# Out-projection of a hybrid decoder trunk: PSUM banks opened with the residual, and a sixth pair of K tiles by seven products

## Chip, cores and metric

The kernel runs on one core of a Trainium2 chip. The metric is device microseconds of one launch, the median of several runs. The engines are TensorE (PE; its weight loads PEld), VectorE (DVE), ScalarE (ACT), GpSimd (POOL), and SyncE (SP), which issues nearly all DMAs.

## What is computed

Two layers, 256 tokens, width 2048, all in float32. In each layer (the reference, cut to what matters):

```python
h  = rmsnorm(x, attn_norm_g[l])
P  = h @ w_in[l]                       # q | k | v | gate_B | gate_C | conv_in
A  = differential_attention(...)       # 8 heads, 1024 columns
Cv = gate_B * short_conv(gate_C * conv_in)         # 1024 columns
x  = x + concat([A, Cv]) @ w_out[l]    # 2048 x 2048
x  = x + relu(rmsnorm(x, mlp_norm_g[l]) @ w_up[l]) ** 2 @ w_down[l]
```

## The kernel before

Tokens make two tiles of 128 (t = 0, 1), output columns make chunks of 512. A float32 product is made of three products of rounded halves (high·high, high·low, low·high: `TERMS`). Each weight tile is therefore loaded raw by SP, rounded to a high part by ScalarE (`whi`) and subtracted to a low part by VectorE (`wlo`). Raw tiles have four buffers (`RAW`), the pairs `whi`/`wlo` three, and `Weights.take` makes tiles three jobs ahead of their use (`AHEAD`).

The out-projection has K = 2048, in 8 pairs of K tiles (i = 0 to 7; 0 to 3 are attention, 4 to 7 convolution). It is done in two halves of the output columns: `left` (chunks 0 and 1) and `right` (chunks 2 and 3). A pair of K tiles and two chunks against two token tiles is a 2x2 by 2x2 block product. It is done in one of two ways:

- *ordinary*, by `pair`: each half is an entry (chunk, i) of the order list, one weight tile of 128 x 2 x 512 and 2 K tiles x 2 token tiles x 3 terms = 12 matmuls of 512 columns; both chunks take 24;
- *by seven*, by `product`: seven products of three matmuls instead of eight, on sums and differences of the blocks. The activations' sums are made once by `sums_of` (`sv`, then high and low part, `sf` or `sg`); the weights' sums by `BySeven.jobs`: two raw tiles, `w7b` and half a `whi`/`wlo` from them directly, four differences `w7t`, of which two give `w7x` and two `w7y`. Each such tile again has a high part from ScalarE and a low part from VectorE. VectorE's operations for one seven are L916, L917, L921, L922 (`w7t`) and four low parts of L880.

The seven products collect in banks `prods[1]` to `prods[7]`; `prods[2]`, `prods[3]`, `prods[4]` and `prods[8]` are also the four places of the output (chunk, token tile) = (0,0), (1,0), (0,1), (1,1), on which the ordinary halves collect. After the last seven `results` combines the banks: ScalarE copies product 1 (L972), VectorE adds (L973 to L976). Its inner `add` (L980) adds four results to the residual `xs` later; a last step adds the four output banks to it (L1061 on the left, L1167 on the right).

The order of the work on TensorE is that of the program (a manual schedule for TensorE alone). On the left it follows the list `LEFT`: columns of the gate ("c", i), the first four products of a seven ("a", i), its last three ("b", i), and ordinary halves (chunk, i). On the right it is `RIGHT`, where ("s", i) is a whole seven. On VectorE, ScalarE and SP a scheduler sets the order; each engine then runs its queue in order. The right half is followed by the MLP, whose weights come by L1284 (`uraw`, 1 MB each from w_up) and L1302 (`draw`).

Of the kernel before, what the change touches and what calls it, by code (L numbers as in the profile page):

```python
# [9 lines left out]
F32 = mybir.dt.float32  # L10
F32R = mybir.dt.float32r
AF = mybir.ActivationFunctionType
# [3 lines left out]
P = 128  # L16
# [3 lines left out]
NT = S // P  # L20
# [8 lines left out]
CH = 512  # L29
# [28 lines left out]
TERMS = ((0, 0), (0, 1), (1, 0))  # L58
# [75 lines left out]
def trunk(ctx: ExitStack, tc: tile.TileContext, x, w_in, w_out, conv_w, q_norm_g, k_norm_g,  # L134
          lambda_q1, lambda_k1, lambda_q2, lambda_k2, subln_g, attn_norm_g, mlp_norm_g,
          w_up, w_down, rel_bias, selector, out):
    nc = tc.nc
# [696 lines left out]
    A11, A21, A12, A22, S1, S2, S3, S4 = range(8)  # L834

    class BySeven:
# [9 lines left out]
        def sums_of(self, i, a11, a21, a12, a22):  # L846

            if i < self.rooms_of:
                if i % 2 == 0 or not self.rooms:
                    room = self.pool.tile([P, 2, 2, 4, P], F32R, tag="b", name="sf")  # L850
                    self.rooms = [room[:, 0], room[:, 1]]
                hi, lo = (self.rooms[i % 2][:, part] for part in range(2))
            else:
                hi, lo = (self.tmp.tile([P, 4, P], F32R, tag="s", name="sg", bufs=2)
                          for _ in range(2))
            self.sums[i] = hi, lo
            v = wide(f"sv{i}").rearrange("p (s c) -> p s c", c=P)
            nc.vector.tensor_add(v[:, 0], a21, a22)
# [4 lines left out]
            nc.vector.tensor_sub(lo, v, hi.bitcast(F32))  # L863
# [74 lines left out]
        def product(self, n, i, a, b, start, stop):  # L938

            for m, (pa, pw) in enumerate(TERMS):  # L940
                nc.tensor.matmul(self.prods[n], self.form(i, pa, a), b[pw],  # L941
                                 start=(start and m == 0), stop=(stop and m == 2))

        def pair(self, i, chunks, starts=(), last=False):

            for n, accs in chunks:
                hi, lo = self.weights.take()
                for j in range(2):
                    k = 2 * i + j
                    a = self.cat[k // KG]  # L950
                    while not a.ready:
                        work.tick()
                    steps = [(t, pa, pw) for t in range(NT) for pa, pw in TERMS]
                    if self.weights.ramp and self.weights.used == 1 and j == 0:
                        steps = [(t, pa, pw) for pa, pw in ((0, 0), (1, 0), (0, 1))
                                 for t in range(NT)]
                    for t, pa, pw in steps:
                        nc.tensor.matmul(  # L958
                            accs[t], a.ap[:, pa, k % KG, t * P:(t + 1) * P], (hi, lo)[pw][:, j],
                            start=(j == 0 and (pa, pw) == (0, 0) and (n, t) in starts),  # L960
                            stop=(last and j == 1 and (pa, pw) == TERMS[-1]))
                    work.tick()

        def results(self, n):


            prods = self.prods
            x11, x21, x12, x22 = (xs[n + m][:, t] for m in range(2) for t in range(NT))
            room = self.tmp.tile([P, 2, CH], F32, tag="ao", name="es", bufs=1)
            e1, e2, e3 = room[:, 0], wide("e2"), room[:, 1]  # L970
            e4 = self.kpool.tile([P, CH], F32, tag="kL", name="es4")
            nc.scalar.activation(e1, prods[1], AF.Copy)  # L972
            nc.vector.tensor_add(e2, prods[6], e1)  # L973
            nc.vector.tensor_add(e4, prods[5], e2)
            nc.vector.tensor_add(x22, prods[5], x22)
            nc.vector.tensor_add(e3, prods[7], e2)  # L976

            def add():
                for x_, e in ((x11, e1), (x21, e3), (x12, e4), (x22, e3)):
                    nc.vector.tensor_add(x_, x_, e)  # L980

            return add

        def left_jobs(self, w_gate, col, w):

# [12 lines left out]
        def left(self, acts, cv):  # L998
# [21 lines left out]
            def banks():  # L1020
                for a, b in ((1, 6), (2, 3)):
                    w2 = mm.tile([P, NT, CH], F32, tag="mm2", name=f"po{l}{a}")
                    prods[a], prods[b] = w2[:, 0], w2[:, 1]
                for n in (5, 7, 4):
                    prods[n] = bank(f"po{l}{n}")

            for j, (what, i) in enumerate(LEFT):
                start, end = i == SEVEN_LEFT[0], i == SEVEN_LEFT[-1]
                rest = {w for w, _ in LEFT[j + 1:]}
                if what == "c":  # L1030
                    column(i)
                elif what == "a":
                    if start:
                        banks()
                    b11, b21, b22 = weights.take()
                    self.t1, self.t3 = weights.take()
                    self.product(1, i, A11, b11, start, end)
                    self.product(2, i, A12, b21, start, not {"a", 0} & rest)
                    self.product(3, i, S4, b22, start, not {"a", 1} & rest)
                    self.product(5, i, S1, self.t1, start, end)  # L1040
                    work.tick()
                elif what == "b":
                    t2, t4 = weights.take()
                    self.product(7, i, S3, self.t3, start, end)
                    self.product(6, i, S2, t2, start, end)
                    self.product(4, i, A22, t4, start, not {"b", 0} & rest)
                    work.tick()
                    if end:
                        add = self.results(0)
                else:  # L1050
                    opening = what == 1 and 8 not in prods
                    if opening:
                        prods[8] = ps.tile([P, CH], F32, tag="av", name=f"po{l}8", bufs=1)
                    accs = ((prods[2], prods[4]), (prods[3], prods.get(8)))
                    self.pair(i, [(what, accs[what])], [(1, 1)] if opening else (),
                              not {what, "b"} & rest)
# [88 lines left out]
        def right(self, norm):  # L1145

            weights, l = self.weights, self.l
            both = [mm.tile([P, NT, CH], F32, tag="mm2", name=f"o{l}{n}") for n in (2, 3)]
            accs = [[acc[:, t] for t in range(NT)] for acc in both]
            self.prods = prods = {2: accs[0][0], 4: accs[0][1], 3: accs[1][0]}  # L1150
            opened, add = set(), None

            for j, (what, i) in enumerate(RIGHT):
                rest = {w for w, _ in RIGHT[j + 1:]}
                if what == "s":
                    self.seven(i, i == SEVEN_RIGHT[0], i == SEVEN_RIGHT[-1], rest)
                    if i == SEVEN_RIGHT[-1]:
                        add = self.results(2)
                    continue
                first = what not in opened  # L1160
                opened.add(what)
                self.pair(i, [(what, accs[what])],
                          [(what, t) for t in range(NT)] if first else (),
                          not {"s", what} & rest)
                if not {"s", what} & rest:
                    for t in range(NT):
                        nc.vector.tensor_add(xs[2 + what][:, t], accs[what][t], xs[2 + what][:, t])  # L1167
                    if add is not None:
                        add()
                        add = None  # L1170
                    work.start(norm.chunk(2 + what, 2), 0 if what else 2)


# [579 lines left out]
```

## Time and profile before

| what | value |
|---|---|
| runs | 2112.37, 2112.66, 2113.86 us; median 2112.66 |
| span of the profiled execution | 2110.7 us |
| TensorE busy | 2105.2 us, at full granted clock throughout |
| VectorE, ScalarE, GpSimd busy | 1834.6, 1407.5, 189.4 us |
| left half from the first seven on, layer 1 | 251.8 to 336.6 us |
| right half, layer 1 | 336.6 to 375.2 us |

The profile shows one execution; its span runs from the first to the last instruction, and no other time of that execution is given. The runs' times contain what lies around the span. In rows of instructions the first number is the start and the second the duration, both in us; square brackets hold the idle time ahead of an instruction and what ended it. Rows of groups give the busy time in all, the mean in ns, and the idle time ahead.

### The profile page before, as it was taken

The page shows a single profiled execution, that of the slowest core. Times are in us where ns is not written, and L with a number is a line of the kernel's source. Part 1 is how long each engine was busy: PE and PEld are TensorE (multiplying, and loading weights), DVE is VectorE, ACT ScalarE, POOL GpSimd, SP SyncE. Part 2 cuts the span into 40 slices and gives each one's busy share as a digit, 9 for nine tenths or more (in the row PEclk, how much of TensorE's full clock was granted, in tenths as well). Part 3 has the DMA queues.
Part 4 walks back from the last instruction along what each step waited for, and adds up shares of the span by engine and source line. Part 5 has one row for each costly group of instructions (what it writes and reads, how often), then busy time and mean ns, then how long its engine had stood idle before and what let it go on. Part 6 is the DMA issues. An engine that isn't in the chain of part 4 may idle for free.

```text
span 2110.7 us, 29252 instructions
## 1 busy us (share of the span) xinstructions
PE 2105.2 (100%) x10809; PEld 1799.0 (85%) x10809; DVE 1834.6 (87%) x2525; ACT 1407.5 (67%) x1823; POOL 189.4 (9%) x226
## 2 busy tenths in 40 slices
PE   9999999999999999999999999999999999999999
PEld 7888888888888888888888888888888888888887
DVE  7888788898888888799888887988988888888998
ACT  6777566676776766666566775657676677675664
POOL 2211120000000000011101121000000000000110
PEclk9999999999999999999999999999999999999999
DMA  7655575887777777789566456668777777777993
GB/s 265 205 154 167 171 216 182 289 259 229 230 238 229 231 232 230 251 291 310 171 220 188 152 170 185 195 193 290 255 238 229 229 230 238 230 229 260 315 309 113
DMA packets 312607, 476.01 MB, mean 226 GB/s; under 512 B 12723, under 2 KB 209669, under 8 KB 312464
## 3 DMA queue, kind: packets, MB, share of 16 engines
q1 hardware_dynamic: 284752, 406.76, 60.7%
q0 software_dynamic: 27520, 67.24, 10.1%
q8 instruction: 85, 1.39, 0.3%
q14 instruction: 58, 0.48, 0.1%
q10 hardware_dynamic: 192, 0.15, 0.0%
HBM read 440.52 MB, written 33.58 MB: 225 GB/s over the span
## 4 chain that ended last, share of the span: by engine, by line
PE 98%; DMA 1%; POOL 1%; DVE 1%; issue 0%; ACT 0%; ACTq 0%; DVEq 0%
PE upc L1427 31%; PE pr L1470 14%; PE dn L1551 8%; PE gc L481 4%; PE ci L481 4%; PE gb L433 4%; PE v L456 3%; PE q L958 3%; PE o L958 3%; PE k L958 3%; PE dn L1470 3%; PE po L941 2%; PE dn L1645 2%; PE pr1r L1470 2%; PE pr0r L1470 2%; PE po L958 2%
## 5 line engine op out<-in xcount | busy, mean ns | idle before, releaser
L1427 PE MATMUL upc<-nT,uhi 128*128 128x512 f32 x1920 | 454.7, 389 | 0.0
L1427 PEld LDWEIGHTS upc<-nT,uhi 128*128 128x128 f32 x1920 | 360.2, 188 | 74.7
L1292 DVE TENSOR_TENSOR ulo<-uraw,uhi 128x1024 fp32r<-128x1024 f32 x256 | 312.3, 1222 | 109.8 <-ACT f L1459 91.5
L341 ACT ACTIVATE whi<-raw 128x1024 fp32r<-128x1024 f32 x232 | 244.7, 1058 | 180.2 <-issue 21.8
L1291 ACT ACTIVATE uhi<-uraw 128x1024 fp32r<-128x1024 f32 x256 | 270.6, 1057 | 135.7 <-PE upc L1427 115.4
L342 DVE TENSOR_TENSOR wlo<-raw,whi 128x1024 fp32r<-128x1024 f32 x232 | 284.3, 1234 | 53.1 <-ACT whi L341 46.9
L1427 PEld LDWEIGHTS upc<-nT,ulo 128*128 128x128 f32 x1920 | 246.2, 191 | 9.4
L1427 PE MATMUL upc<-nT,ulo 128*128 128x256 f32 x1920 | 249.1, 283 | 0.0
L1317 ACT ACTIVATE bh<-draw 128x1536 fp32r<-128x1536 f32 x86 | 128.3, 1492 | 103.7 <-PE pr L1470 82.1
L1318 DVE TENSOR_TENSOR bl<-draw,bh 128x1536 fp32r<-128x1536 f32 x86 | 151.3, 1759 | 11.4 <-ACT bh L1317 10.9
L1551 PE MATMUL dn<-whi,fb 128*128 128x512 f32 x480 | 152.0, 389 | 0.0
L1470 PE MATMUL pr<-bh,f 128*128 128x512 f32 x360 | 121.4, 391 | 0.0
L341 ACT ACTIVATE whi<-uraw 128x1024 fp32r<-128x1024 f32 x60 | 63.7, 1062 | 72.0 <-PE dn L1551 58.5
L1437 ACT ACTIVATE ev<-upc 128x512 f32<-128x512 f32 x120 | 72.0, 600 | 54.0 <-PE upc L1427 54.0
L1317 ACT ACTIVATE t24h<-t 128x1024 fp32r<-128x1024 f32 x86 | 91.4, 1063 | 23.7 <-PE pr L1470 15.9
L1551 PEld LDWEIGHTS dn<-whi,fb 128*128 128x128 f32 x480 | 90.1, 188 | 18.6
L1318 DVE TENSOR_TENSOR t24l<-t,t24h 128x1024 fp32r<-128x1024 f32 x86 | 104.9, 1220 | 0.2
L1330 DVE TENSOR_TENSOR t<-draw 128x1024 f32<-128x1024 f32 x86 | 105.0, 1221 | 0.1
L1318 DVE TENSOR_TENSOR t13l<-t,t13h 128x1024 fp32r<-128x1024 f32 x86 | 104.9, 1220 | 0.0
L1317 ACT ACTIVATE t13h<-t 128x1024 fp32r<-128x1024 f32 x86 | 91.5, 1063 | 8.1 <-DVE t L1330 2.9
L1470 PE MATMUL pr<-t13h,f 128*128 128x512 f32 x240 | 93.8, 391 | 0.0
L1551 PE MATMUL dn<-wlo,fb 128*128 128x512 f32 x240 | 93.4, 389 | 0.0
(528 smaller groups left out, 4383.9 us busy)
## 6 DMA issues: line engine op xcount, KB each, us to landing
uraw<-in_w_up_dram SPq DMA_DIRECT2D x128, 1024.0 KB, 6.3
raw<-in_w_in_dram SPq DMA_DIRECT2D x191, 512.0 KB, 4.2
draw<-in_w_down_dram SPq DMA_DIRECT2D x180, 512.0 KB, 5.3
raw<-in_w_out_dram SPq DMA_DIRECT2D x64, 512.0 KB, 4.5
uraw<-in_w_down_dram SPq DMA_DIRECT2D x60, 512.0 KB, 6.8
hid0p<-f POOLq DMA_DIRECT2D x17, 512.0 KB, 3.5
fb<-hid0p POOLq DMA_DIRECT2D x17, 512.0 KB, 8.0
hid1p<-f POOLq DMA_DIRECT2D x17, 512.0 KB, 3.5
```

The lines of the kernel that those rows point to most:

```text
L341: pair = (nc.scalar.activation(hi, raw, AF.Copy), nc.vector.tensor_sub(lo, raw, hi.bitcast(F32)))
L342: nc.vector.tensor_sub(lo, raw, hi.bitcast(F32)))
L481: nc.tensor.matmul(acc[:, f, 0] if part else acc[:, f], wt[:, k % 4, fs], a.ap[:, 0, k % KG] if part else a.ap[:, :, k % KG], start=(part ...
L958: nc.tensor.matmul(accs[t], a.ap[:, pa, k % KG, t * P:(t + 1) * P], (hi, lo)[pw][:, j], start=(j == 0 and (pa, pw) == (0, 0) and (n, t) in ...
L1291: pair = (nc.scalar.activation(hi, src, AF.Copy), nc.vector.tensor_sub(lo, src, hi.bitcast(F32)))
L1292: nc.vector.tensor_sub(lo, src, hi.bitcast(F32)))
L1317: keep(nc.scalar.activation(hi, src, AF.Copy))
L1318: keep(nc.vector.tensor_sub(lo, src, hi.bitcast(F32)))
L1330: keep(nc.vector.tensor_sub(t[:, 0:2], raw[:, 0::2], raw[:, 1::-1]))
L1427: nc.tensor.matmul(acc[:, 0] if part else acc, wt[part][:, k], a.ap[:, 0, k % KG] if part else a.ap[:, :, k % KG], start=(part == 0 and kh ...
L1470: nc.tensor.matmul(prods[n], f[:, pa, a], b[pw], start=(start and m == 0), stop=(stop and m == 2))
L1551: nc.tensor.matmul(prods[p], f[:, pa, 2 * k + t], b[pw][:, n], start=(p in starts and k == 0 and m == 0), stop=(stop and k == 1 and m == 2))
```

## The change

Two things are changed. First, the output banks are opened with the residual: a new `seed` has ScalarE copy `xs` into the bank, and all matmuls on it accumulate (no `start`). On the left these are the places of `prods[2]`, `prods[3]` and `prods[8]`, on the right all four. The additions of the residual in `results` go, as does its `add`; results are written to `xs` directly, and the last four additions stay. Second, pair 5 of the left half moves from two ordinary halves to a seven. The seven's last parts now stand among the ordinary halves of pairs 6 and 7. `sums_of` makes the sums of pair 5 in a room of `tmp` that the temporaries of `results` had.

```diff
 LEFT = (("c", 0), ("a", 0), ("c", 1), ("b", 0), ("c", 2), ("a", 1), ("c", 3), ("b", 1),
         ("c", 4), ("a", 2), ("c", 5), ("b", 2), ("c", 6), ("a", 3), ("c", 7), ("b", 3),
-        (0, 5), (1, 5), ("a", 4), ("b", 4), (0, 6), (1, 6), (0, 7), (1, 7))
+        (0, 6), (1, 6), ("a", 4), ("b", 4), (0, 7), ("a", 5), ("b", 5), (1, 7))
...
+            elif i % 2:
+                room = self.tmp.tile([P, 2, 4, P], F32R, tag="ao", name="so", bufs=1)
+                hi, lo = (room[:, part] for part in range(2))
             else:
...
+        def seed(self, *places):
+
+            for n, t, acc in places:
+                nc.scalar.activation(acc, xs[n][:, t], AF.Copy)
 
         def results(self, n):
...
-            room = self.tmp.tile([P, 2, CH], F32, tag="ao", name="es", bufs=1)
-            e1, e2, e3 = room[:, 0], wide("e2"), room[:, 1]
-            e4 = self.kpool.tile([P, CH], F32, tag="kL", name="es4")
-            nc.scalar.activation(e1, prods[1], AF.Copy)
-            nc.vector.tensor_add(e2, prods[6], e1)
-            nc.vector.tensor_add(e4, prods[5], e2)
-            nc.vector.tensor_add(x22, prods[5], x22)
+            e2, e3 = wide("e2"), x21 if n else wide("e3")
+            nc.scalar.activation(x11, prods[1], AF.Copy)
+            nc.vector.tensor_add(e2, prods[6], x11)
+            nc.vector.tensor_add(x12, prods[5], e2)
             nc.vector.tensor_add(e3, prods[7], e2)
-
-            def add():
-                for x_, e in ((x11, e1), (x21, e3), (x12, e4), (x22, e3)):
-                    nc.vector.tensor_add(x_, x_, e)
-
-            return add
+            nc.vector.tensor_add(x22, prods[5], e3)
+            if not n:
+                nc.vector.tensor_add(x21, x21, e3)
...
+                self.seed((0, 0, prods[2]), (1, 0, prods[3]))
...
                         prods[8] = ps.tile([P, CH], F32, tag="av", name=f"po{l}8", bufs=1)
+                        self.seed((1, 1, prods[8]))
...
                     if j == len(LEFT) - 1:
-                        add()
                         for n in range(2):
                             for t in range(NT):
                                 nc.vector.tensor_add(xs[n][:, t], accs[n][t], xs[n][:, t])
...
+            for n in range(2):
+                self.seed(*((2 + n, t, accs[n][t]) for t in range(NT)))
```

The order on the engines changes too. On VectorE, in layer 1, the end of the weights' work for the right half's first seven stood so before (`w7t` and `w7y` belong to that seven, the `wlo` of 128x1024 to ordinary halves, `nT` to the normalised input of the MLP; in the changed kernel lines behind 850 have numbers that differ by up to 4, here by 3):

```order
L921 TENSOR_TENSOR w7t<-w7t,raw 128x512
L880 TENSOR_TENSOR w7x<-w7t,w7x 128x1024
L880 TENSOR_TENSOR wlo<-raw,whi 128x512
L309 SCALAR_TENSOR_TENSOR nT_1_3582<-tpn_0_3587,gains,nT_1_3582 128x256 x2
L922 TENSOR_TENSOR w7t<-raw,w7t 128x512
L309 SCALAR_TENSOR_TENSOR nT_1_3582<-tpn_1_3610,gains,nT_1_3582 128x256 x2
L342 TENSOR_TENSOR wlo<-raw,whi 128x1024
L880 TENSOR_TENSOR w7y<-w7t,w7y 128x1024
L342 TENSOR_TENSOR wlo<-raw,whi 128x1024
```

and on the same engine at the same place it stands so now:

```order
L924 TENSOR_TENSOR w7t<-w7t,raw 128x512
L342 TENSOR_TENSOR wlo<-raw,whi 128x1024
L883 TENSOR_TENSOR w7x<-w7t,w7x 128x1024
L883 TENSOR_TENSOR wlo<-raw,whi 128x512
L309 SCALAR_TENSOR_TENSOR nT_1_3600<-tpn_0_3605,gains,nT_1_3600 128x256 x2
L925 TENSOR_TENSOR w7t<-raw,w7t 128x512
L309 SCALAR_TENSOR_TENSOR nT_1_3600<-tpn_1_3628,gains,nT_1_3600 128x256 x2
L342 TENSOR_TENSOR wlo<-raw,whi 128x1024 x2
L883 TENSOR_TENSOR w7y<-w7t,w7y 128x1024
```

The ordinary low part that stood behind `w7y`, of the half (0, 5), now stands ahead of it.

On VectorE at the end of the left half of layer 1 it stands so now around the sixth seven (`po_2771` and the like are banks, `x_84` and `x_85` the residual of the two chunks):

```order
L883 TENSOR_TENSOR w7x<-w7t,w7x 128x1024
L925 TENSOR_TENSOR w7t<-raw,w7t 128x512
L342 TENSOR_TENSOR wlo<-raw,whi 128x1024
L883 TENSOR_TENSOR w7y<-w7t,w7y 128x1024
L342 TENSOR_TENSOR wlo<-raw,whi 128x1024
L981 TENSOR_TENSOR e_3463<-po_2771,x_84 128x512
L982 TENSOR_TENSOR x_85<-po_2773,e_3463 128x512
L983 TENSOR_TENSOR e_3464<-po_2774,e_3463 128x512
```

The low part ahead of `w7y` is that of the half (0, 0) of the right. In the kernel before no seven stands there; its last left seven was followed by four ordinary halves.

On SP, from the last raw tiles of the left half of layer 1 to the MLP's first ones, it stood so before (`raw` of L383 is a tile of an ordinary half, `raw` of L895 one of a seven):

```order
L383 DMA raw<-in_w_out_dram 128x2x512 x10
L895 DMA raw<-in_w_out_dram 128x2x512 x2
L383 DMA raw<-in_w_out_dram 128x2x512 x2
L895 DMA raw<-in_w_out_dram 128x2x512 x2
L383 DMA raw<-in_w_out_dram 128x2x512 x4
L1284 DMA uraw<-in_w_up_dram 128x8x256 x5
L1302 DMA draw<-in_w_down_dram 128x1024 x6
```

and on SP it stands so now, from the two raw tiles of the sixth left seven:

```order
L898 DMA raw<-in_w_out_dram 128x2x512 x2
L383 DMA raw<-in_w_out_dram 128x2x512 x6
L1282 DMA uraw<-in_w_up_dram 128x8x256 x2
L383 DMA raw<-in_w_out_dram 128x2x512
L898 DMA raw<-in_w_out_dram 128x2x512 x2
L383 DMA raw<-in_w_out_dram 128x2x512 x2
L898 DMA raw<-in_w_out_dram 128x2x512 x2
L383 DMA raw<-in_w_out_dram 128x2x512 x4
L1282 DMA uraw<-in_w_up_dram 128x8x256 x3
```

Two of the MLP's loads moved ahead of 11 raw tiles of the right half, among them those of both its sevens.

More of the change, by code (lines that the diff above doesn't have):

```diff
@@ L941, in product @@
                 nc.tensor.matmul(self.prods[n], self.form(i, pa, a), b[pw],
-                                 start=(start and m == 0), stop=(stop and m == 2))
+                                 start=(start and m == 0), stop=(stop and m == 2),
+                                 skip_group_check=True)
         def pair(self, i, chunks, starts=(), last=False):
@@ L960, in pair @@
                             start=(j == 0 and (pa, pw) == (0, 0) and (n, t) in starts),
-                            stop=(last and j == 1 and (pa, pw) == TERMS[-1]))
+                            stop=(last and j == 1 and (pa, pw) == TERMS[-1]),
+                            skip_group_check=True)
                     work.tick()
+        def seed(self, *places):
+            for n, t, acc in places:
+                nc.scalar.activation(acc, xs[n][:, t], AF.Copy)
         def results(self, n):
@@ L1037, in left @@
                     self.product(1, i, A11, b11, start, end)
-                    self.product(2, i, A12, b21, start, not {"a", 0} & rest)
-                    self.product(3, i, S4, b22, start, not {"a", 1} & rest)
+                    self.product(2, i, A12, b21, False, not {"a", 0} & rest)
+                    self.product(3, i, S4, b22, False, not {"a", 1} & rest)
                     self.product(5, i, S1, self.t1, start, end)
@@ L1048, in left @@
                     if end:
-                        add = self.results(0)
+                        self.results(0)
                 else:
@@ L1053, in left @@
                         prods[8] = ps.tile([P, CH], F32, tag="av", name=f"po{l}8", bufs=1)
+                        self.seed((1, 1, prods[8]))
                     accs = ((prods[2], prods[4]), (prods[3], prods.get(8)))
-                    self.pair(i, [(what, accs[what])], [(1, 1)] if opening else (),
-                              not {what, "b"} & rest)
+                    self.pair(i, [(what, accs[what])], (), not {what, "b"} & rest)
                     if j == len(LEFT) - 1:
-                        add()
                         for n in range(2):
@@ L1150, in right @@
             self.prods = prods = {2: accs[0][0], 4: accs[0][1], 3: accs[1][0]}
-            opened, add = set(), None
+            for n in range(2):
+                self.seed(*((2 + n, t, accs[n][t]) for t in range(NT)))
             for j, (what, i) in enumerate(RIGHT):
@@ L1157, in right @@
                     if i == SEVEN_RIGHT[-1]:
-                        add = self.results(2)
+                        self.results(2)
                     continue
[L1160 to L1164, printed above, removed]
+                self.pair(i, [(what, accs[what])], (), not {"s", what} & rest)
                 if not {"s", what} & rest:
```

3 lines of the change are left out of this document (removed).

## The prediction

> **What bounds the kernel now.** I read the page first: its span, busy times, granted clock and chain of waits.
>
> ```profile
> span 2110.7 us, 29252 instructions
> PE 2105.2 (100%) x10809; PEld 1799.0 (85%) x10809; DVE 1834.6 (87%) x2525; ACT 1407.5 (67%) x1823; POOL 189.4 (9%) x226
> PEclk9999999999999999999999999999999999999999
> PE 98%; DMA 1%; POOL 1%; DVE 1%; issue 0%; ACT 0%; ACTq 0%; DVEq 0%
> ```
>
> TensorE is busy for the whole span at the full granted clock, and the chain that ended last is TensorE. The median of the runs, 2112.66 us, is the span plus 1.96; I take that offset as constant and add changes of the span to the median. A measurement can tell about 0.2% (4.2 us) from no change.
>
> Next, TensorE's waits over the whole program, all four that there are:
>
> ```profile
> PE warm L189 <- DVE mhalf L181: 1.1, 1, 1.1
> PE q L958 <- ACT whi L368: 0.4, 1, 0.4
> PE tpb L570 <- DMA x<-in_x_dram: 0.2, 1, 0.2
> PE k00tp L688 <- DVE ke L660: 0.2, 1, 0.2
> ```
>
> None is in the out-projection, so no wait there can be removed. Then the busy time of each engine (window, its length, then TensorE, its weight loads, VectorE, ScalarE, GpSimd) in the left half from the first seven to the end, and in the right half, for each layer:
>
> ```profile
> 251.80:336.60 84.80, 84.80 (x436) 72.53 (x435) 78.23 (x110) 50.16 (x63) 13.66 (x1) 1.00 0.63 195
> 336.60:375.20 38.60, 38.60 (x179) 31.98 (x178) 33.22 (x43) 23.87 (x35) 0.00 (x0) 1.00 0.60 187
> 1301.00:1385.70 84.70, 84.70 (x435) 72.64 (x435) 78.69 (x110) 49.58 (x62) 1.88 (x1) 1.00 0.64 196
> ```
>
> TensorE fills both. VectorE has 84.80 − 78.23 = 6.6 us to spare on the left, 5.4 on the right; ScalarE has 35. So a matmul saved is time saved, and VectorE is the engine to watch.
>
> **Fewer matmuls.** A seven is 7 products of 3 matmuls, 21; an ordinary pair is 2 chunks of 12, 24. One more pair by seven saves 3 matmuls a layer, 6 in all. Their price, and the need of the first seven on the right, are read from its rows on TensorE:
>
> ```profile
> 354.58 0.39 PE L958 MATMUL o<-whi,cat 128*128 128x512 f32 x1
> 354.81 0.84 PE L941 MATMUL po0r<-w7b,cat 128*128 128x512 f32 x3
> 356.85 1.52 PE L941 MATMUL po0r<-w7x,sf 128*128 128x512 f32 x6
> 358.21 0.84 PE L941 MATMUL po0r<-w7y,sf 128*128 128x512 f32 x3
> ```
>
> Six matmuls begin in 358.21 − 356.85 = 1.36 us, 0.227 each (the 0.39 is a duration that overlaps the next). This kernel is bound by that spacing, so the gain is 6 × 0.227 = 1.36 us. The Trainium skill, "TensorE: Matmul & The Clock Gate", section "Back-to-back issue gap", gives about 131 ns a matmul of 512 columns in a sustained stream, by which the gain would be an estimated 0.8 us; the 0.227 of this trace decides.
>
> **More work for VectorE on the left.** What a seven costs there is read from the second one on the right, whose operations follow each other:
>
> ```profile
> 358.67 0.69 DVE L916 TENSOR_TENSOR w7t<-raw 128x512 f32<-128x512 f32 x1 [1.03 <-DMA raw<-in_w_out_dram]
> 363.96 1.22 DVE L342 TENSOR_TENSOR wlo<-raw,whi 128x1024 fp32r<-128x1024 f32 x1
> 365.24 1.23 DVE L880 TENSOR_TENSOR w7y<-w7t,w7y 128x1024 fp32r<-128x1024 f32 x1
> 366.38 1.22 DVE L342 TENSOR_TENSOR wlo<-raw,whi 128x1024 fp32r<-128x1024 f32 x1
> L858 DVE TENSOR_TENSOR sv<-ay 128x128 f32<-128x128 f32 x8 | 2.3, 289 | 0.0
> L863 DVE TENSOR_TENSOR sg<-sv,sg 128x512 fp32r<-128x512 f32 x2 | 1.4, 684 | 0.0
> ```
>
> From 358.67 to 366.38 are 7.71 us, with one ordinary low part (363.96 to 365.24, 1.28) among them: 6.43 for a seven. It replaces two ordinary low parts of 1.13 (start to start, rows below): +4.17. Pair 5 now needs its sums: four of 0.29 and one of 0.68, +1.84. Three additions of 128x512 go (12 become 9), each 0.60 from start to start:
>
> ```profile
> 326.59 0.69 DVE L973 TENSOR_TENSOR e<-po,es 128x512 f32<-128x512 f32 x1
> 327.19 0.69 DVE L980 TENSOR_TENSOR x<-x,es 128x512 f32<-128x512 f32 x1
> 325.23 0.60 ACT L972 ACTIVATE es<-po 128x512 f32<-128x512 f32 x1 [0.44 <-PE po L941]
> ```
>
> That is −1.8, together +4.2 of VectorE's 6.6 − 0.7 (the left is 3 matmuls shorter): 1.7 us remain. On the right four additions go, −2.4. On average it fits, and costs nothing while its queue runs ahead of need; if that cover is gone, what misses is paid one to one.
>
> **The seeds.** ScalarE gains 7 copies of 128x512 a layer into banks, which no row here shows. The nearest is the copy out of a bank above, 0.60, so 4.2 us on an engine with 35 to spare. Bounds: nothing, or all that stands between a bank's release and its first matmul. The tight one is the right half's first bank: the sixth product ends 15 matmuls (3.40 us) before the left ends; ahead of the seeds may stand one low part (1.13), one addition (0.60) and two copies (1.2), 2.9. I take nothing, with 0.5 to spare. The other seeds have more.
>
> **The two tight places.** The order of VectorE now puts an ordinary low part ahead of the last one (w7y) of the sixth left seven and of the right's first seven. That low part waits for ScalarE's high part, which waits for TensorE to release its buffer at the start of the seven. Before, it stood behind w7y:
>
> ```profile
> 355.06 1.06 ACT L341 ACTIVATE whi<-raw 128x1024 fp32r<-128x1024 f32 x1 [0.51 <-PE o L958]
> 346.52 0.68 DVE L916 TENSOR_TENSOR w7t<-raw 128x512 f32<-128x512 f32 x1
> 354.15 1.22 DVE L342 TENSOR_TENSOR wlo<-raw,whi 128x1024 fp32r<-128x1024 f32 x1
> 355.28 1.22 DVE L880 TENSOR_TENSOR w7y<-w7t,w7y 128x1024 fp32r<-128x1024 f32 x1
> 341.29 1.23 DVE L342 TENSOR_TENSOR wlo<-raw,whi 128x1024 fp32r<-128x1024 f32 x1 [1.97 <-ACT whi L341]
> 340.21 1.04 ACT L341 ACTIVATE whi<-raw 128x1024 fp32r<-128x1024 f32 x1
> ```
>
> The release lets ScalarE start 0.25 after the seven's first matmul (355.06 against 354.81); high part 1.06; hand-over 0.04 (341.25 to 341.29); low part 1.13; w7y 1.22: 3.70 us. TensorE wants w7y's low part with the second matmul on it, the 17th, after 16 × 0.227 = 3.63. What a hand-over to TensorE costs shows at the left's last seven, where VectorE is late already:
>
> ```profile
> 323.19 1.22 DVE L880 TENSOR_TENSOR w7y<-w7t,w7y 128x1024 fp32r<-128x1024 f32 x1
> 324.26 0.93 PE L941 MATMUL po<-w7y,sg 128*128 128x512 f32 x3
> 325.03 0.85 PE L941 MATMUL po<-w7y,cat 128*128 128x512 f32 x3
> ```
>
> w7y ends at 324.41; the three matmuls take 0.77 instead of 0.68 to the next three, so the second began at about 324.57, 0.16 behind it. So 3.70 + 0.16 − 3.63 = 0.23 us of waiting at each place; bounds: nothing (if ScalarE's release comes a little sooner) and 1.13 + 0.16 = 1.3 (if a further low part gets in between).
>
> **SP's queue.** Two loads of 1 MB for the MLP now stand ahead of the raw tiles of (1,4), of both sevens on the right and of the halves behind them. The first waits for w7y of the sixth seven, the second for the sixth product.
>
> ```profile
> uraw<-in_w_up_dram SPq DMA_DIRECT2D x128, 1024.0 KB, 6.3
> raw<-in_w_out_dram SPq DMA_DIRECT2D x64, 512.0 KB, 4.5
> uraw<-in_w_up_dram SPq DMA_DIRECT2D x3, 1024.0 KB, 9.0
> ```
>
> One such load lands in 6.3 us, of three in a row (the last row, issued from 369.9) the middle one after 9.0; 1 MB costs 9.0 − 6.3 = 2.7, 512 KB 1.35 (or 6.3 − 4.5 = 1.8 by the two sizes). Issued 3.8 us before the left's end, the second lands 5.2 after it, and the three raw tiles behind it, up to the right's first seven, 9.2 to 10.6 after it. Before, VectorE began on that tile (346.52) 9.9 after the left's end (336.60). From there to the end of w7y (356.50) it worked without a gap, 9.98 us, and was 358.44 − 356.50 = 1.94 early. Now w7b (1.14) and the low part (1.13) lie in that stretch too: 1.94 − 2.27 − 0.16 = −0.49. With the same landing this is 0.49 us of waiting, in place of the 0.23 there; with the landings above, 0.23 to 1.2. I take 0.49.
>
> **The sum.** −1.36 + 2 × (0.23 + 0.49) = +0.1 us: **2112.8**, no change that can be told.
>
> **Rivals.**
> - *Nothing waits* (17%): the queues run a little ahead of what I have them do. Against it: 0.1 us decides at two places. −1.36: 2111.3.
> - *VectorE runs out on the left* (17%): its 1.7 us to spare cannot be moved to the last 15 us, where two sevens stand with one half between. For it: it is 0.09 late there already. Against it: a seven and a half take TensorE 33 × 0.227 = 7.5 us and VectorE 7.6. If 1 us a layer is missed: −1.36 + 2 × (1 + 0.49) = +1.6: 2114.3.
> - *The MLP's loads starve the right half* (12%; slower). The raw tiles share one queue with 2 MB ahead of them; if they land 3 us later than the 9.9 above, every operation of VectorE on the first seven moves by that: 2 × (0.23 + 0.49 + 3) − 1.36 = +6.1: 2118.8. It decides over 0.2% from a landing 2.1 us later, 12.0 after the left's end, when 2 × (0.72 + 2.1) − 1.36 = 4.3. For it: nothing of VectorE's lead is left. Against it: the sum of landings gives 10.6 at most. The Trainium skill, "DMA: Bandwidth & Descriptors", section "Queues, rings and completion order", says that each DMA engine consumes the descriptors of a ring in order, and that SP owns one ring on each; by that, nothing behind the 2 MB can overtake it. That three loads in a row land later one by one agrees.
> - *More gain than the six matmuls* (4%): only by waits that the four rows above don't show; −4.3 or more.
>
> My forecast holds the other 50%. Its own range is 2111.3 to 2114.9: both tight places at nothing, or the first at its upper bound (−1.36 + 2 × (1.3 + 0.49) = +2.2). The **range** of all is 2111.0 to 2116.5: nothing waiting, with 0.3 us of spread between runs, to a landing about 2 us late. Left out are the worse half of the starving case and the gain, some 14%. Faster by over 0.2%: 0.04; slower: 0.12; between: 0.84.
>
> **What would show it.** Six matmuls fewer; TensorE's waits with new rows of a few tenths at the sixth seven and at the right's first, on w7y from VectorE. If the right's first seven waits for over 1 us, the idle time of VectorE ahead of its first operation there names the DMA, and the landing is beyond 12 us from the left's end. If TensorE waits for a seed on ScalarE, my 0.5 us to spare was wrong. A left half longer than 84.8 − 0.7 + 0.2 us makes VectorE the bound there.

## The result and the profile after

The changed kernel takes 2116.93 us, median of 20 runs (2114.82 to 2118.83); the kernel before takes 2112.60 (2112.12 to 2113.86, 20 runs). The ratio is 1.002, with an interval of 1.0013 to 1.0027: 4.3 us slower, where 0.1 was forecast and 2116.5 was the end of the range. The runs also scatter over 4.0 us instead of 1.7.

The page of the changed kernel: span, busy times and the chain of waits.

```profile
span 2114.3 us, 29264 instructions
PE 2106.5 (100%) x10803; PEld 1798.4 (85%) x10803; DVE 1837.1 (87%) x2533; ACT 1416.3 (67%) x1843; POOL 176.8 (8%) x226
PE 93%; DVE 2%; DMA 2%; issue 1%; POOL 1%; ACT 1%; ACTq 0%; DVEq 0%
```

Six matmuls are gone (10809 to 10803), the span is 3.6 us longer, and 5% of the chain has passed from TensorE to VectorE, DMA and others. TensorE's waits that the changed kernel has and the kernel before had not (the view names a part of each; the gaps between matmuls are some tenths longer):

```profile
PE po0r L944 <- DVE w7y L883: 0.9, 1, 0.9
PE po1r L944 <- DVE w7y L883: 0.9, 1, 0.9
PE o L962 <- DVE wlo L342: 0.4, 1, 0.4
PE tpn L528 <- DVE tot L582: 0.3, 1, 0.3
```

They stand on the right half's first seven (`po0r`, `po1r`), at the half (1, 4) ahead of it (`o`), and at the MLP's first input (`tpn`). The windows of the changed kernel from first matmul to first matmul of each stage show where the time went (window; length; TensorE's busy time): left from its first seven, right up to its first seven, and right from there to the MLP, for layer 1, then the same for layer 2. The left is counted here from the first matmul of the first seven, 257.39 in the kernel before; the 251.8 of the table ahead of the prediction is the first matmul of the gate's columns, 5.6 us earlier.

```profile
257.72:336.57 78.85, 78.77 (x401) 67.03 (x399) 75.05 (x107) 49.17 (x64) 1.88 (x1) 1.00 0.69 207
336.57:355.50 18.93, 18.50 (x90) 15.01 (x89) 15.11 (x23) 14.09 (x26) 0.00 (x0) 1.00 0.68 240
355.50:382.94 27.44, 26.53 (x119) 21.62 (x118) 22.05 (x26) 13.78 (x18) 0.00 (x0) 1.00 0.61 197
1308.55:1387.31 78.76, 78.76 (x401) 67.03 (x399) 74.68 (x107) 48.64 (x64) 1.88 (x1) 1.00 0.70 208
1387.31:1405.91 18.60, 18.52 (x89) 15.01 (x88) 15.13 (x23) 14.10 (x26) 0.00 (x0) 1.00 0.70 239
1405.91:1433.31 27.40, 26.52 (x119) 21.62 (x118) 21.77 (x26) 13.55 (x18) 0.00 (x0) 1.00 0.65 197
```

Against the same marks of the kernel before, whose stages are 79.2, 18.2 and 26.2 us long in layer 1 and 79.1, 18.2 and 26.2 in layer 2:

| change, us | left | right, to its first seven | right, from it | up to the MLP's next stage | sum |
|---|---|---|---|---|---|
| layer 1 | −0.36 | +0.71 | +1.25 | +0.05 | +1.65 |
| layer 2 | −0.36 | +0.39 | +1.19 | +0.49 | +1.71 |

With +0.3 us of ordinary scatter ahead of layer 1's left half that is the 3.65 between the last matmuls. The right half pays 3.5 of it.

How the first seven on the right came to wait, in layer 1 of the changed kernel. SP's DMA instructions around the end of the left half (start and duration; where two are merged, from the start of the first to the end of the last), and the DMAs issued from 331 to 343 with their size and the time from issue to landing (the first load, the raw tile issued ahead of it at 331.27, the second load, and the three raw tiles behind):

```profile
332.57 1.11 SPq L1282 DMA_DIRECT2D uraw<-in_w_up_dram  x2
333.77 3.61 SPq L383 DMA_DIRECT2D raw<-in_w_out_dram  x1
339.74 2.70 SPq L898 DMA_DIRECT2D raw<-in_w_out_dram  x2
uraw<-in_w_up_dram SPq DMA_DIRECT2D x1, 1024.0 KB, 8.6
raw<-in_w_out_dram SPq DMA_DIRECT2D x1, 512.0 KB, 6.0
uraw<-in_w_up_dram SPq DMA_DIRECT2D x1, 1024.0 KB, 10.6
raw<-in_w_out_dram SPq DMA_DIRECT2D x1, 512.0 KB, 11.5
raw<-in_w_out_dram SPq DMA_DIRECT2D x1, 512.0 KB, 6.8
raw<-in_w_out_dram SPq DMA_DIRECT2D x1, 512.0 KB, 5.7
```

The two 1 MB loads, issued 332.57 and 333.31, land at 341.2 and 343.9; the three raw tiles behind them at 345.3, 346.5 and 347.8. One follows the other: what is behind the 2 MB lands behind them. VectorE, ScalarE and TensorE at the same place:

```profile
347.88 0.69 DVE L919 TENSOR_TENSOR w7t<-raw 128x512 f32<-128x512 f32 x1 [1.99 <-DMA raw<-in_w_out_dram]
351.61 1.22 DVE L342 TENSOR_TENSOR wlo<-raw,whi 128x1024 fp32r<-128x1024 f32 x1
356.60 1.06 ACT L341 ACTIVATE whi<-raw 128x1024 fp32r<-128x1024 f32 x1 [3.23 <-DMA raw<-in_w_out_dram]
356.65 2.35 DVE L342 TENSOR_TENSOR wlo<-raw,whi 128x1024 fp32r<-128x1024 f32 x2
358.92 1.22 DVE L883 TENSOR_TENSOR w7y<-w7t,w7y 128x1024 fp32r<-128x1024 f32 x1
358.89 0.39 PE L944 MATMUL po0r<-w7y,sf 128*128 128x512 f32 x1
360.19 0.74 PE L944 MATMUL po0r<-w7y,sf 128*128 128x512 f32 x2 [0.91 <-DVE w7y L883]
```

VectorE waits 2.0 us for the raw tile and begins the seven's sums 347.88 − 336.57 = 11.3 us after the left's end; before, it was 9.9 without a wait. The low part of the half (1, 4) stands behind four operations of the seven (351.61), so that half waits 0.7. It gives its raw buffer back late, so the next raw tile comes late too (356.60), and `w7y`, behind that tile's low part, ends at 360.14. TensorE's second matmul on it begins at 360.19 instead of 359.12.

### The profile page after: what moved, and what is told of

Its sections match the earlier page's. It is cut to its first block, busy times and chain, and to the rows that moved or that the text cites. A ratio compares the mean times of both kernels' runs of the same rounds, so it can differ in the third digit from the quotient of the medians.

```text
span 2114.3 us, 29264 instructions
## 1 busy us (share of the span) xinstructions
PE 2106.5 (100%) x10803; PEld 1798.4 (85%) x10803; DVE 1837.1 (87%) x2533; ACT 1416.3 (67%) x1843; POOL 176.8 (8%) x226
## 4 chain that ended last, share of the span: by engine, by line
PE 93%; DVE 2%; DMA 2%; issue 1%; POOL 1%; ACT 1%; ACTq 0%; DVEq 0%
PE upc L1425 31%; PE pr L1468 14%; PE dn L1549 8%; PE gc L481 4%; PE ci L481 4%; PE gb L433 4%; PE v L456 3%; PE q L962 3%; PE k L962 3%; PE dn L1468 3%; PE po L944 2%; PE dn L1643 2%; PE pr1r L1468 2%; PE pr0r L1468 2%; PE upw L1425 1%; PE o L962 1%
## 5 line engine op out<-in xcount | busy, mean ns | idle before, releaser
L342 DVE TENSOR_TENSOR wlo<-raw,whi 128x1024 fp32r<-128x1024 f32 x228 | 278.6, 1230 | 47.9 <-ACT whi L341 40.7
L1316 DVE TENSOR_TENSOR bl<-draw,bh 128x1536 fp32r<-128x1536 f32 x86 | 151.3, 1759 | 11.4 <-ACT bh L1315 10.9
```

The source lines that it names most:

```text
L342: nc.vector.tensor_sub(lo, raw, hi.bitcast(F32)))
L1316: keep(nc.vector.tensor_sub(lo, src, hi.bitcast(F32)))
```

## Experiments

Two theories. A: the MLP's two loads in front make the right half's raw tiles land late, and this adds to what the order of the low parts takes. B: the order of the low parts makes the waits by itself. Each kernel was timed in alternation with the kernel before on the same chip. "Landing" is the start of the first operation on the seven's raw tiles (L919; L925 or L916 in other numberings) after the right's first matmul.

**Loads behind.** Two temporaries of `results` keep their old rooms until the right half's end:

```diff
-            e2, e3 = wide("e2"), x21 if n else wide("e3")
+            room = self.tmp.tile([P, 2, CH], F32, tag="ao", name="es", bufs=1)
+            e2, e3 = room[:, 0], self.kpool.tile([P, CH], F32, tag="kL", name="e3")
...
-                    nc.vector.tensor_add(xs[2 + what][:, t], accs[what][t], xs[2 + what][:, t])
+                    nc.vector.tensor_add(xs[2 + what][:, t], accs[what][t],
+                                         e3 if (what, t) == (0, 1) else xs[2 + what][:, t])
```

> The changed kernel with the MLP's first loads put back behind all raw tiles of the right half, by keeping two temporaries of results in the rooms they had before, up to the right half's end. No instruction is added, and VectorE's order up to the right half's second seven stays that of the changed kernel. Theory A (the two 1 MB loads in front make the right half's raw tiles land late, and all of VectorE's work there stands behind that): VectorE's wait for the raw tile ahead of L919 (2.0 us in layer 1 after the change) goes, the wait ahead of the right's first seven (0.4 to 0.7 us at the half before it) goes, and that on w7y falls from 1.1 to 0.3-0.5; each layer gains about 1.2, time 2114.5 us. Theory B (the order of the low parts makes the waits, the landing is only a bystander): the wait on w7y stays at 1 us or more, time 2116 us or more.

Measured 2113.75 us (2112.28 to 2114.78; ratio 1.0004, 0.9996 to 1.0013). Its windows of layer 1, left and right in the two parts, the sums' start and `w7y`:

```profile
257.55:336.66 79.11, 78.72 (x400) 67.02 (x399) 74.73 (x107) 48.88 (x63) 1.88 (x1) 1.00 0.68 210
336.66:354.88 18.22, 18.22 (x90) 15.09 (x89) 16.28 (x26) 14.32 (x26) 0.00 (x0) 1.00 0.45 130
354.88:381.30 26.42, 26.42 (x120) 21.62 (x118) 20.98 (x24) 13.90 (x18) 0.00 (x0) 1.00 0.75 244
346.09 0.70 DVE L919 TENSOR_TENSOR w7t<-raw 128x512 f32<-128x512 f32 x1
357.31 1.22 DVE L883 TENSOR_TENSOR w7y<-w7t,w7y 128x1024 fp32r<-128x1024 f32 x1
```

The wait for DMA is gone, landing is 9.4, and the right half is 0.2 us longer than before instead of 2.0, with VectorE's order unchanged. Against the kernel before on each chip the loss falls from 4.3 to 1.05 us, so some 3.3 go: A, and more of it than the 2.4 expected; B by itself had 2116 us or more. What stays is on the left, 0.66 and 0.40 us at the sixth seven in the two layers.

**w7y first.** High and low part of the half after a seven's last sums are queued behind these, on both sides:

```diff
+                made = two(room, mine["t"][:, 2:4])
+                if self.rooms_of == 4:
+                    self.weights.hold = self.last
...
+                with ExitStack() as order:
+                    for ins in self.hold:
+                        order.enter_context(tc.issue_after(ins.ins))
                     pair = (nc.scalar.activation(hi, raw, AF.Copy),
                             nc.vector.tensor_sub(lo, raw, hi.bitcast(F32)))
+                self.hold = ()
```

> The changed kernel with the ordinary low part (and its high part) that follows a seven's last weight sums in the program kept behind them on VectorE and ScalarE; the MLP's loads stay ahead of the right half's raw tiles. Theory A (landing): VectorE still waits 1.5-2 us for the raw tile, the half before the right's first seven still waits 0.3-0.7 and w7y is still late by some tenths, while the wait of 0.3 at the sixth left seven goes: 2115 us. Theory B (order): the waits on w7y go at both places, the right half is back at its length before (44.4 us) and time is 2116.9 - 2 x (0.3 + 1.1) = 2114 us or less.

**Both**, the two edits together:

> The loads behind and w7y first, together. If the two causes are all there is, nothing waits in the out-projection: 2112.6 - 1.4 = 2111.3 us, below the kernel before by 0.06%. If VectorE's six low parts and sums more on the left are a cause of their own, waits stay on the left and the time is 2112.5 us or more.

Measured 2121.13 us (1.0046, 1.0032 to 1.0059) and 2118.45 us (1.0028, 1.0017 to 1.0039): slower than the changed kernel, which no theory had. Waits of TensorE with both, and the rows on ScalarE at the left's end:

```profile
PE o L971 <- ACT o L981: 4.5, 2, 2.3
336.75 1.06 ACT L345 ACTIVATE whi<-raw 128x1024 fp32r<-128x1024 f32 x1 [2.80 <-PE po L971]
337.71 1.22 ACT L981 ACTIVATE o<-x 128x512 f32<-128x512 f32 x2
```

The edit let a high part slip ahead of the seeds of the right's first bank on ScalarE. That high part waits for TensorE's last half (2.80), the seeds wait behind it, and TensorE waits for the seeds, 2.3 us a layer by the view and 2.4 from matmul to matmul. So these two runs say nothing on A and B, but they show the third tight place: the 0.5 us that the prediction had there holds only for the order that the changed kernel has.

**Sevens only.** Before's `results` and no seeds, with the new left list and the room "so":

```diff
-        (0, 5), (1, 5), ("a", 4), ("b", 4), (0, 6), (1, 6), (0, 7), (1, 7))
+        (0, 6), (1, 6), ("a", 4), ("b", 4), (0, 7), ("a", 5), ("b", 5), (1, 7))
...
+            elif i % 2:
+                room = self.tmp.tile([P, 2, 4, P], F32R, tag="ao", name="so", bufs=1)
```

> The kernel before with the sixth left seven and the new order of the left list, but without the seeds: results and its additions as before, so the MLP's loads stay behind the right half's raw tiles. Theory A (landing, which comes from the seeds' rewriting of results): right half as in the kernel before or up to 0.5 us longer, left half 0.3-1 us above its 79.2 - 0.7, time 2112-2114 us. Theory B (order): VectorE's low parts stand in the changed kernel's order at the right's first seven, one ahead of w7y, so about 1 us is waited there, 2114-2116 us.

Measured 2113.74 us (1.0005, 0.9996 to 1.0014), in A's band. The left is +0.29 and −0.41 us, the right +0.22 and +0.69. The run does not test B as was meant, for VectorE's order is not that of the changed kernel: between the last `w7t` of the right's first seven and its `w7y` stands one ordinary low part, where the changed kernel has two. It does test the prediction's balance (0.49 us plus what the landing is beyond 9.9). The landings were 10.7 and 11.1 us even with the loads behind: the tile took only 3.7 and 4.0 us from its issue, but was issued later, because VectorE gave the buffer back later. Less one low part of 1.13 the balance gives 0.2 and 0.6, near the 0.22 and 0.69 of the right.

**Seeds only.** The changed kernel with the old left list (the same line of `LEFT` the other way round):

> The kernel before with the seeds and the new results, but with five sevens on the left in the old order. The MLP's first two loads come ahead of the right half's raw tiles here too, one after the other, but their rooms come free some 8 us earlier (at w7y of the fifth seven), and VectorE has as many operations ahead of w7y on the right as before. Theory A (the right half waits by what the raw tile's landing is later than 9.9 us after the left's end, plus what the order adds): landing near 10, no wait, 2112.7 us, the same as before within 0.5. Theory C (the seeds themselves cost: ScalarE's copies into banks delay high parts): a wait on ScalarE at the right's first matmul, 0.5-1 us a layer, 2114 us.

Measured 2114.98 us (1.0010, 1.0001 to 1.0019): slower, against A's 2112.7 as I had worked it out, and in C's size. But the rows are not C's. Waits of TensorE, ScalarE's rows ahead of the seeds of the right's second bank, and the raw tiles whose issue falls between 328 and 332:

```profile
PE o L962 <- ACT o L972: 1.8, 1, 1.8
338.84 1.06 ACT L341 ACTIVATE whi<-raw 128x1024 fp32r<-128x1024 f32 x1 [3.83 <-DMA raw<-in_w_out_dram]
343.73 0.58 ACT L972 ACTIVATE o<-x 128x512 f32<-128x512 f32 x1
raw<-in_w_out_dram SPq DMA_DIRECT2D x2, 512.0 KB, 10.9
```

The raw tiles behind the two loads take 10.9 us, a high part waits 3.83 for one, and the seeds stand behind it in ScalarE's queue. In layer 1 that costs 3.8 us, in layer 2 nothing. The wait itself is 1.8 of the 3.8; most of the rest is TensorE's clock, of which more below. The traced execution, 2116.41 us, is one of the slowest of the 11. It is the landing again, at another place.

**One load ahead.** One temporary keeps its old room, so one load is put back; the other stays ahead of the seven's raw tiles:

```diff
-            e2, e3 = wide("e2"), x21 if n else wide("e3")
+            room = self.tmp.tile([P, 2, CH], F32, tag="ao", name="es", bufs=1)
+            e2, e3 = room[:, 0], x21 if n else self.kpool.tile([P, CH], F32, tag="kL", name="e3")
```

> The changed kernel with one of the MLP's two loads put back behind, and one left ahead of the raw tiles of the right's first seven (behind that of the half before it). Theory A (landing): the raw tile lands about 2.7 us sooner than the 11.0 to 11.3 of the changed kernel, so no later than the 9.4 with both behind by much: right half 0 to 0.6 us longer than before, time 2113.7-2114.7 us, between loads_behind (2113.75) and the changed kernel (2116.9), nearer the former. Rival: one load in front is enough to hold the queue, and the time is 2116 us or more.

Measured 2119.14 us (1.0030, 1.0018 to 1.0041): not between the two, but worse than either. The expectation was wrong in sign; the rival beside it, 2116 us or more, came out.

```profile
339.71 0.37 SPq L1283 DMA_DIRECT2D uraw<-in_w_up_dram  x1
340.79 2.70 SPq L898 DMA_DIRECT2D raw<-in_w_out_dram  x2
350.77 0.69 DVE L919 TENSOR_TENSOR w7t<-raw 128x512 f32<-128x512 f32 x1 [3.05 <-DMA raw<-in_w_out_dram]
```

Its room comes free only after the left's end, so the load goes out at 339.71, straight ahead of the raw tiles that are needed next. Landing is 13.2 us, the right half 3.0 us longer in each layer; in this execution the left halves are longer too, by 1.05 and 0.13. It counts how near ahead a load stands, not only how many there are.

**w7y first, right only.** As w7y first, for the sevens of the right half alone:

```diff
-                if self.rooms_of == 4:
+                if self.rooms_of == 4 and not in_keys:
                     self.weights.hold = self.last
```

> The changed kernel with one thing moved: on the right half's sevens the low part (and high part) of the half behind them stands behind w7y. The MLP's loads stay ahead, and the left half's order is that of the changed kernel. Theory A (late landing and order add up: 0.49 us and what the landing is beyond 9.9 us): of 1.55 to 1.9 us on the right 1.13 goes, 0.4 to 0.8 a layer remain, most of it at the half before the seven (0.3 to 0.7), time 2116.9 - 2 x 1.13 = 2114.7 us. Order alone: the right half waits for nothing, 2113.5 us or less. Landing alone: right half as in the changed kernel, 2116.9 us.

Measured 2115.46 us (1.0014, 1.0005 to 1.0022), between the theories, 0.8 above A's 2114.7. The landings of the two layers are 10.7 and 11.7:

```profile
349.23 0.69 DVE L925 TENSOR_TENSOR w7t<-raw 128x512 f32<-128x512 f32 x1 [1.36 <-DMA raw<-in_w_out_dram]
1399.71 0.69 DVE L925 TENSOR_TENSOR w7t<-raw 128x512 f32<-128x512 f32 x1 [2.42 <-DMA raw<-in_w_out_dram]
```

Nothing waits on the `w7y` of the right's first seven. The expectation took one low part of 1.13 out of the balance; in the trace both low parts that stood ahead of `w7y` are gone, 2.26, so the balance leaves no wait there in layer 1 and 0.1 us in layer 2, and that agrees. The right waits at places that the balance does not have: 0.07 and 1.14 us up to the first seven, at the half ahead of it, and 0.6 to 0.7 a layer further on, part of it at the second seven. In this execution the left half of layer 1 is 1.87 us longer than before as well: its fifth seven waits some 1.6 us for `w7y`, its sixth 1.0.

**Untangled.** Loads behind, w7y first for the sixth left seven (i == 5) and the right ones, and the seeds of the right's first bank right behind `results` of the left:

```diff
                         self.results(0)
+                        self.first_out = mm.tile([P, NT, CH], F32, tag="mm2", name=f"o{l}2")
+                        self.seed(*((2, t, self.first_out[:, t]) for t in range(NT)))
...
-            for n in range(2):
-                self.seed(*((2 + n, t, accs[n][t]) for t in range(NT)))
+            self.seed(*((3, t, accs[1][t]) for t in range(NT)))
```

> The change with its three costs taken out together: the MLP's loads behind the right half's raw tiles; w7y ahead of the ordinary low parts behind it at the sixth left seven and at the right's sevens; and the seeds of the right's first bank written right behind results in the program, so that no high part that waits for TensorE stands ahead of them on ScalarE. If the causes are complete: nothing waits in the out-projection, left half 0.68 us shorter than before, right as before, some 0.2 us a layer at the MLP's start; 2112.7 - 1.4 + 0.4 = 2111.7 us. If VectorE is simply out of time on the left, a wait of 0.3 us or more stays at the sixth seven: 2112.5 us or more.

Measured 2111.85 us (0.9997, 0.9988 to 1.0006) against 2112.49 for the kernel before on that chip, 0.2 from the forecast. TensorE's waits in the whole program, none of them in the out-projection:

```profile
PE warm L189 <- DVE mhalf L181: 1.1, 1, 1.1
PE q L971 <- ACT whi L373: 0.4, 1, 0.4
PE tpb L575 <- DMA x<-in_x_dram: 0.3, 1, 0.3
257.25:335.68 78.43, 78.43 (x400) 67.11 (x399) 75.11 (x107) 49.26 (x63) 1.88 (x1) 1.00 0.68 207
1305.89:1384.33 78.44, 78.44 (x401) 67.11 (x399) 74.39 (x107) 48.89 (x63) 1.88 (x1) 1.00 0.68 208
```

The rows of windows are the left halves: 78.43 us, 0.77 and 0.68 shorter than before, three matmuls. The right halves are as long as before to 0.01 us. So six sevens' work does fit on VectorE.

**Loads ahead, order mended.** Untangled without the first of its edits:

> As untangled, but with the MLP's two loads left ahead of the right half's raw tiles, as in the changed kernel (the first of them two raw tiles further ahead). Theory A: the left half stays 0.68 us shorter than before; the raw tile lands about 11 us after the left's end, of 0.49 + 1.1 - 1.13 = 0.5 us of waiting a layer on the right, so 2111.85 + 2 x 0.5 = 2112.8 us, and a right half whose waits follow the landing from run to run. Rival: with the order mended the loads' place is worth nothing, 2111.9 us.

Measured 2116.99 us (1.0022, 1.0013 to 1.0031; 2114.86 to 2120.24). The order is mended, the left is 0.67 us shorter in both layers, and the loads' place costs 5.2 us against the next run; the first load stands two raw tiles further ahead than in the changed kernel. Waits of TensorE, the landings of layers 1 and 2, and the DMAs issued from 331 to 345:

```profile
PE o L971 <- DVE wlo L346: 2.9, 1, 2.9
349.81 0.69 DVE L925 TENSOR_TENSOR w7t<-raw 128x512 f32<-128x512 f32 x1 [3.31 <-DMA raw<-in_w_out_dram]
1399.28 0.69 DVE L925 TENSOR_TENSOR w7t<-raw 128x512 f32<-128x512 f32 x1 [0.92 <-DMA raw<-in_w_out_dram]
raw<-in_w_out_dram SPq DMA_DIRECT2D x5, 512.0 KB, 9.2
uraw<-in_w_up_dram SPq DMA_DIRECT2D x1, 1024.0 KB, 12.9
```

Landing is 13.8 us in layer 1, where TensorE loses 4.7 us ahead of the seven, and 10.2 in layer 2, where it loses nothing there. My 11 was no constant: in one execution the same loads in the same order gave both.

Of the 4.7 us only 3.1 are the wait. Behind it the granted clock was 0.50 up to 358.03 and matmuls began every 0.43 us instead of 0.23 (window; length, TensorE's busy time and matmuls, granted clock, share and GB/s of the DMA engines):

```profile
354.81:358.03 3.22, 3.22 (x8) 0.50 0.55 165
358.03:361.44 3.41, 3.41 (x17) 1.00 0.80 282
```

That is 1.6 us on top of the wait. It is not in every run: seven of the 11 have a mean granted clock of 1.000, the other four 0.999, so the median's 5.2 us do not rest on it. All 20 runs of the changed kernel have 1.000.

**Untangled again**, beside it:

> The kernel of untangled once more, on the same chip as the run above, for the interval: 2111.3 to 2112.3 us against the kernel before on that chip.

Measured 2111.82 us (0.9996, 0.9987 to 1.0005) against 2112.61: the same as at first. Both medians are 0.6 to 0.8 us below the kernel before; both intervals contain 1, so that it is faster is not settled. That the changed kernel's loss is gone is. The medians keep about half of the 1.36 us of the six matmuls; where the other half goes is not shown, since each trace is of one execution, the first of them the fastest of its 11.

## Why the prediction failed

- **The six matmuls** were right: 0.68 us a layer, which the traced execution of untangled gets in full.
- **VectorE on the left** fits on average, with more to spare than worked out: 78.85 − 75.05 = 3.8 us in layer 1 of the changed kernel, not 1.7. No wait over 0.2 us stays when its queue is ordered for it.
- **The sixth left seven** was predicted at 0.23 us of waiting; 0.35 and 0.27 were measured in the changed kernel. In other runs with the same order there it was 0.25 to 1.03 (right only: 1.03 and 0.25). That part of the VectorE rival is true; a lasting lack of time is not. What moves VectorE's queue there by some tenths no run settles.
- **The seeds** cost nothing in the changed kernel, as predicted, but only while nothing slow stands ahead of them on ScalarE.
- **SP's queue is the step that failed**, the size of a term. I let the second load land 5.2 us after the left's end, the raw tile by 10.6 at most, and took 9.9. Measured: the second load goes out 3.3 us ahead of the end, not 3.8, and takes 10.6 us instead of 9.0. It lands 7.4 after the end, and VectorE begins on the tile at 11.3 (layer 2: 11.0). The steps behind the first load were right: 2.7 us to the second, 1.2 to 1.3 to each raw tile (1.35 in the prediction). What was too short is the first load's own time, 8.6 us in place of 6.3. The raw tile issued 1.3 us ahead of it was still under way (6.0 us to landing); that this is the reason is not shown, since with one load ahead a load issued 0.6 us after the last raw tile had landed took 8.4 as well. The balance built on it holds: 0.49 + 11.3 − 9.9 = 1.9 and 0.49 + 11.0 − 9.9 = 1.6, measured 1.96 and 1.58 for the right half. With these in place of 0.49 the sum is −1.36 + 2 × 0.23 + 1.9 + 1.6 = +2.6 us; 0.2 more at the sixth left sevens, 0.5 at the MLP's starts and 0.3 of scatter ahead of layer 1 make it the 3.65 of the profile. So the landing makes 2.5 of the 4.2 us by which the forecast missed. With it alone the time would have been 2115.2, inside the range; the small terms that the sum had at nothing, and a median 0.8 us above the traced execution (2116.14), put it outside.
- **A number that is a spread** was used as a number. Between 10.2 and 13.8 us were measured with two loads ahead. Where VectorE has no lead, a later landing goes to TensorE nearly one to one (11.3 and 11.0 us made 1.96 and 1.58). The 4 us of scatter between the runs may come from that; with one execution traced it is not shown. The starving rival, from 12.0 on, had this mechanism, and its 12% were too few.
- **A place was missed**: the wait also falls on the half ahead of the seven, whose low part stands behind the seven's first sums.

The shares, each against the kernel before on its chip: loads ahead about 3.3 us (5.2 with the order mended), the orders on VectorE and ScalarE with the left's waits about 1.7 (loads behind against untangled, 1.05 and −0.64), six matmuls −1.36 by the traces. The last is only half there in the medians, so the shares do not add up exactly to 4.3. Why the same loads cost 3.3 with one order and 5.2 with the other is not shown; a left half that waits gives the landing more time, which may be part of it.

Not settled: why the 2 MB take 7 us once and 10 us another time. No run changed what else the DMA engines do at that moment.

## What to carry to other kernels

When a change frees a buffer early, look for the transfer that waits for this buffer: a scheduler sends it at once, and what is behind it on the same queue lands behind it, which cost 3.3 to 5.2 us here. Hold the room until the urgent loads are out. Where an engine's queue has no lead left, work out its waits from the worst landing in the trace, not from the median, and look for work that waits for another engine ahead of the short step that the bound engine needs.

## What the hardware showed that I had not expected

An instruction that issues a DMA can hold its engine. The raw tile's instruction right behind the two 1 MB loads took 3.61 us on SP (layer 2: 3.71) where each other one there takes 0.37; with the order mended it was 4.70 (layer 2: 1.56), with seeds only 3.8. No such time stands at that place in the kernel before. It cost nothing here, for the next tile waited for its buffer until 339.7. Why SP is held is not shown: with one load ahead the instruction behind the load took 0.37.

All transfers landed in the order of their issue: SP's 645 DMAs, in every run. The Trainium skill, "DMA: Bandwidth & Descriptors", section "Queues, rings and completion order", has each DMA engine take descriptors in ring order; the landings above (341.2, 343.9, 345.3, 346.5, 347.8) agree. The section does not say that transfers also end in that order, so the prediction's "nothing behind the 2 MB can overtake it" goes further than its source, and holds here by the landings.

A long wait of TensorE can be paid twice. Behind three waits, of 1.8 us (seeds only, layer 1), 2.3 (w7y first, layer 1) and 2.9 (order mended, layer 1), the granted clock was 0.5 for 3.4 us, which is 1.7 us of work at full clock. Behind three others of 2.3 us (w7y first, layer 2, and both, in both layers) it stayed at 1.0, as behind those of up to 1.5. What decides between them no run shows.
